# Gate and up with the first weight row's sign turned, s3 and s4 of the early pairs summed by accumulating transfers, and some changes in the mixers

## The chip, the cores and the metric

The kernel runs on one core of a Trainium2 chip. A core has a matrix engine (TensorE, PE), a vector engine (VectorE, DVE), an engine for activations and copies (ScalarE, ACT), a programmable one (GpSimd, POOL) and one that here only issues transfers (SyncE, SP). Each engine runs its own instructions in order and waits on semaphores for the others. Transfers issued by POOL can add to what stands in the destination; those issued by SP copy. The metric is the time of one execution on the device in microseconds (us).

## The reference

A two-layer encoder is applied to 512 + 256 tokens of width 1024 with shared weights. Cut to what matters:

```python
def rmsnorm(x, g):
    y = x32 * lax.rsqrt(jnp.mean(x32 * x32, axis=-1, keepdims=True) + EPS)
    return y.astype(x.dtype) * g
def swiglu(h, wg, wu, wd):
    return (jax.nn.silu(h @ wg) * (h @ wu)) @ wd
def even_layer(x, ...):
    x = x + 0.5 * swiglu(rmsnorm(x, f1_n), f1_g, f1_u, f1_d)
    x = x + mixer_ab(rmsnorm(x, mix_n), ...)
    x = x + 0.5 * swiglu(rmsnorm(x, f2_n), f2_g, f2_u, f2_d)
def odd_layer(x, ...):
    # the same with mixer_c in the middle
```

`mixer_ab` is a gated mixing of 128-token blocks (gelu, layer normalization, a 128x128 mixing matrix for each of four groups) beside attention in windows with 8 heads; `mixer_c` is attention in a 2-D neighbourhood with 16 heads and a bias from a table. The hidden width of the four FFNs (`swiglu`) is 2816. A normalization follows the last layer. All is float32.

## The kernel before

**Numbers.** A float32 product is made of three matmuls of a rounded type: each operand is split into `hi` (a cast on ScalarE, L125 for weights, L211 for activations) and `lo` (source minus hi, on VectorE, L126 and L212); then hi x hi, hi x lo and lo x hi are summed (`mm3`, L191).

**FFN.** The 768 tokens are two halves of 384. The hidden width is cut into 11 pairs of two 128-row blocks. For each pair, gate and up are made by a 2x2 scheme with seven instead of eight block products (Winograd's form of Strassen's): weight blocks a11 to a22 (columns of a pair's block i, upper or lower half of the 1024 inputs), activation blocks b11 to b22. The weight sums are s1 = a21 + a22, s2 = s1 - a11, s3 = a11 - a21, s4 = a12 - s2; the activation sums are t1 = b12 - b11, t2 = b22 - t1, t3 = b22 - b12, n4 = b21 - t2 (`feed_tmp`, `feed_t2`, `rest`, `combine`). The products are a11 b11, a12 b21, s2 t2, s3 t3, a22 n4, s1 t1, s4 b22. A product is 12 matmuls of 384 columns. The down projection (`down`, L797) uses the same scheme over two pairs at a time, with s3 of its own.

**Pairs and order.** The first four pairs (`EARLY`) of each FFN are split: their products a11 b11 and a12 b21 come first for all four, while the rest of the normalized input is still being made; the other five are done in `settle` (L681), pair after pair, in the order t2, t3, n4, t1, b22, gate then up. `entry` (L672) loads the weights of such a pair again, four transfers of 512 KB on SP, and `added` (L664) builds s1 by two transfers on POOL for each of gate and up, the second of which adds. s2, s3 and s4 are made by VectorE in `sums` (L771, at L773). `entry` of a pair runs at the end of the pair before it for pairs 1 and 2; for pair 3 it runs at its own start, after `down` of pairs 0 and 1 (L749). In the second FFN, the first after a mixer, L750 to L753 emit ahead of this point 60 transfers on POOL (L1668 and L1673: `skew`, 16 and 32, and `tab`, 8 and 4) that build the tables of the second mixer's bias.

**Order on the engines.** TensorE's order is that of the program. The other engines' orders are made by a scheduler when the program is built: of what is ready at a point of its own reckoning it takes what is earliest in the program, `high_priority` moves instructions ahead, and `issue_after` puts one behind another. On the chip each engine then follows its list strictly. Weight tiles `raw` have four buffers, sums `s` eight, `whi` and `wlo` five each.

**Mixers and norms.** `rsqrt` (L318) makes an inverse root either by about a dozen small VectorE instructions (L325 to L336) or, with `power`, by one on VectorE and one power on POOL (L322, L323). In the first mixer (L1158) `attention` and the gating run as side chains beside the projections: `turn` transposes and splits probabilities, `values` copies and adds halves of an output (L1282, L1288), `sgu` normalizes (L1350), splits, mixes and writes (L1359). Their results lie in four banks of the second accumulator pool (`ps_aux`).

Of the kernel before, what the change touches and what calls it, by code (L numbers as in the profile page):

```python
# [47 lines left out]
WTOTAL = 12 * D * FF + 16 * EARLY * P * D + D * 1792 + 2 * D * D + D * 3072 + D * 512  # L48
# [7 lines left out]
class Trunk:  # L56
# [43 lines left out]
    def raw(self, name, k0, nk, c0, n, raw=None, eng=None, **kw):  # L100
        i = len(self.units)
        self.units.append((name, k0, nk, c0, n))
        size = P * nk * n
        src = self.aps["w"][self.woff : self.woff + size].rearrange("(p f) -> p f", p=P)
        self.woff += size
        if raw is None:
            raw = self.rawp.tile([P, nk * n], F32, tag="raw", name=f"raw{i}")
        ins = (eng or self.nc.sync).dma_start(raw, src, **kw).ins  # L108
        if kw:
            self.added = ins  # L110
        else:
            self.loading = ins
        return raw.rearrange("p (k n) -> p k n", k=nk)
# [95 lines left out]
    def split(self, hi, lo, src, eng=None):  # L209
        nc = self.nc  # L210
        nc.scalar.copy(hi, src)  # L211
# [31 lines left out]
    def norm_tok(self, acc, c0, c1):  # L243
# [8 lines left out]
        self.rsqrt(y, ps[:, :nb], 1.0 / D, sm[:, 0, :nb], sm[:, 2, :nb], it[:, :nb])  # L252
# [9 lines left out]
    def tok_norm(self, h):  # L262
# [149 lines left out]
    def gain_split(self, n, k, src, m):  # L412

        hi, lo = self.b[n][k]
        ins = self.nc.scalar.activation(hi, src, AF.Copy, scale=self.gain(m)).ins
        self.fed = ins, self.nc.vector.scalar_tensor_tensor(
            out=lo, in0=src, scalar=self.gain(m), in1=hi.bitcast(F32), op0=ALU.mult, op1=ALU.subtract
        ).ins

    def combine(self, out, x, sign, m, other):  # L420

        g, op = (self.gain(m), ALU.subtract) if sign > 0 else (self.gain(m, self.ngains), ALU.add)
        self.nc.vector.scalar_tensor_tensor(out=out, in0=x, scalar=g, in1=other, op0=ALU.mult, op1=op)  # L423

    def rest(self, *after):
# [7 lines left out]
        for n in ("t3", "n4", "t1", "b22"):  # L433
            for k in range(4):
                with ExitStack() as stack:
                    for ins in self.holds:
                        stack.enter_context(self.tc.issue_after(ins))
                    if n == "t1":
                        self.gain_split(n, k, self.tmp[k], k)
# [4 lines left out]
                    elif n == "n4":  # L444
                        t = self.tmp["t2", k]
                        self.combine(t, self.x[k + 4][:, a0:a1], 1, k + 4, t)
# [48 lines left out]
    def ffn(self, pre):  # L495
# [49 lines left out]
        def pair(p):  # L545
# [15 lines left out]
            def sums(n, name):  # L561
                return self.sums(a[n, 1, 1], a[n, 1, 2], a[n, 2, 1], a[n, 2, 2], s, n, name)
# [39 lines left out]
            def hidden(i, half, g, u):  # L602
# [6 lines left out]
                nc.scalar.activation(t, t, AF.Silu)  # L609
                self.freed = nc.vector.tensor_tensor(out=v, in0=u, in1=r, op=ALU.mult).ins  # L610
                nc.vector.scalar_tensor_tensor(out=t, in0=t, scalar=0.5, in1=v, op0=ALU.mult, op1=ALU.mult)
# [51 lines left out]

            def added(then=None):  # L664
# [7 lines left out]
            def entry(ahead=False):  # L672
                if not loaded:
                    load((0, 1))
# [6 lines left out]
            def settle(st):  # L681
# [3 lines left out]
                for i, (n, b) in enumerate(todo):  # L685
# [14 lines left out]
                    if n == "up":  # L700
                        if b == "n4":
# [69 lines left out]
    def sums(self, a11, a12, a21, a22, s, n, name):  # L771
# [4 lines left out]
        if name == "s2" and (n, "s1") in s:  # L776
            t = s[n, "s2"] = self.fw.tile([P, 4, P], F32, tag="s", name="s2", bufs=8)
            f(t, s[n, "s1"], a11, ALU.subtract)
            return t
        if name == "s4":  # L780
            t = s[n, "s2"]
            f(t, a12, t, ALU.subtract)
# [5 lines left out]
        if name == "s3":  # L788
            f(t, a11, a21, ALU.subtract)
        else:  # L790
            f(t, s[n, "s1"], a11, ALU.subtract)
# [198 lines left out]
    def norm_r(self, mp, cols):  # L990
# [9 lines left out]
        self.ry = self.norm_tok(acc, 0, T)  # L1000
# [157 lines left out]
    def mixer0(self):  # L1158
# [104 lines left out]
        def turn(kv, n, blks, p):  # L1263
            res = []
            for i, b in enumerate(blks):
# [6 lines left out]
                res.append((th, tl))  # L1272
            return res

        def values(kv, n, blks, tt):
# [6 lines left out]
            nc.scalar.copy(tb, po[64:128, :])  # L1282
            for r in range(4):
                o = ot[4 + 2 * kv + r // 2]
                out, rows = o[r % 2 * 64 : r % 2 * 64 + 64, n * P : (n + 1) * P], lambda v: v
                if kv:
                    out, rows = self.by_column(o, slice(r % 2 * 64, r % 2 * 64 + 64), n * P, (n + 1) * P)
                nc.vector.tensor_tensor(  # L1288
                    out=out, in0=rows(po[0:64, r * P : (r + 1) * P]), in1=rows(tb[:, r * P : (r + 1) * P]), op=ALU.add
                )  # L1290
# [43 lines left out]
        def stats(vs):  # L1334
# [8 lines left out]
            self.rsqrt(y, mv[:, 0:3, 1], 1.0, nb, mv[:, 5, 0:3], it)  # L1343
# [3 lines left out]
        def sgu(n, v, y, nb):  # L1347

            i = n % 3
            nc.scalar.activation(v, v, AF.Identity, scale=y[:, i : i + 1], bias=nb[:, i : i + 1])  # L1350
            yield SGU[0] + i * SGU[1]
# [5 lines left out]
            for g in range(4):  # L1357
                c = slice(g * P, (g + 1) * P)
                nc.vector.scalar_tensor_tensor(  # L1359
                    out=ot[g][:, n * P : (n + 1) * P], in0=ps[:, c], scalar=lng[:, g : g + 1], in1=sb[:, c],  # L1360
                    op0=ALU.mult, op1=ALU.add,
                )
# [503 lines left out]
```

## Time and profile before

| what | value |
|---|---|
| median of three runs | 2585.51 us (2584.96 to 2587.59) |
| the profiled execution | 2584.44 us, its span 2582.7 us |
| mean granted TensorE clock | 0.997 |
| moved by transfers | 238.69 MB, of it 22.42 MB by POOL's queue |

A row of the page's groups gives line, engine, operation, output and input tiles, shape and count, then busy time, mean ns of one, and idle time of the engine just before it with what ended most of it. A row of the waits gives the engine and tile that waited, for whom, and the us in total, times, and longest. A row of the timeline gives start, length and the instruction, in brackets the idle time before it and who ended it. A row of stretches gives its bounds and length, then the busy time and count of PE, PEld, DVE, ACT and POOL, the granted clock, the share of the transfer engines and GB/s. The last number of a transfer's row is the time in us from issue to landing.

### The profile page before, as it was taken

Reading aid. Unit: us, or ns where it says so; the run is one execution under the profiler, and the core shown is the slowest. Engines: PE = TensorE matmul, PEld = TensorE weight load, DVE = VectorE, ACT = ScalarE, POOL = GpSimd, SP = SyncE. Lnnn points to the kernel's source line nnn. Section 1 sums busy time; section 2 is a strip of 40 time slices with the busy share of each in tenths; the row PEclk is TensorE's granted clock in tenths of the full one; section 3 lists DMA queues with packets and bytes.
Section 4 is the critical chain, followed back from the end, with each engine's and each line's share of the span. In section 5 each row is a group of like instructions: output and inputs, shape, how many; then the busy total and the mean of one; then the engine's idle time right before and its main releaser. Section 6 shows DMA issues by size and latency. Waiting matters only on the chain.

```text
span 2582.7 us, 41323 instructions
## 1 busy us (share of the span) xinstructions
PE 2549.8 (99%) x15114; PEld 2485.1 (96%) x15114; DVE 2229.4 (86%) x4650; ACT 1365.0 (53%) x2869; POOL 191.4 (7%) x318
## 2 busy tenths in 40 slices
PE   8999999999999999999999999999999999999998
PEld 8999999987899999999999999998998999999997
DVE  7988899888879889889998889986767699988897
ACT  7544454555656545445654445454545465444543
POOL 1000000000020500000100000001222220000000
PEclk9999999999999999999999999999999999999999
DMA  7422222421234722222532222242221343222222
GB/s 255 121 82 66 82 66 66 158 74 46 62 115 131 202 66 80 68 77 88 143 103 82 66 82 66 66 146 64 64 64 41 106 143 111 82 77 72 74 67 73
DMA packets 79422, 238.69 MB, mean 92 GB/s; under 512 B 9969, under 2 KB 18993, under 8 KB 79217
## 3 DMA queue, kind: packets, MB, share of 16 engines
q1 hardware_dynamic: 69136, 213.32, 25.9%
q0 software_dynamic: 9792, 22.42, 4.0%
q8 instruction: 119, 1.95, 0.3%
q14 instruction: 87, 0.70, 0.1%
q10 hardware_dynamic: 288, 0.29, 0.0%
HBM read 226.56 MB, written 15.07 MB: 94 GB/s over the span
## 4 chain that ended last, share of the span: by engine, by line
PE 88%; DVE 8%; ACT 2%; DMA 1%; issue 1%; DVEq 0%; ACTq 0%; POOL 0%; POOLq 0%
PE ps_mm L155 53%; PE ps_aux L155 33%; DVE wlo L126 1%; DMA raw<-in_w 1%; PE ps_aux L159 1%; ACT p L1143 1%; DVE p L1137 1%; DVE tmp L423 0%; DVE tl L212 0%; DVE p L1153 0%; ACT whi L125 0%; DVE s L773 0%; DVE o L1288 0%; DMA tok<-in_xt 0%; PE ps_aux L1719 0%
## 5 line engine op out<-in xcount | busy, mean ns | idle before, releaser
L125 ACT CAST whi<-s 128x512 fp32r<-128x512 f32 x496 | 304.7, 620 | 409.3 <-DVE s L773 185.8
L125 ACT CAST whi<-raw 128x512 fp32r<-128x512 f32 x504 | 306.5, 619 | 225.8 <-PE ps_mm L155 92.3
L126 DVE TENSOR_TENSOR wlo<-s,whi 128x512 fp32r<-128x512 f32 x496 | 337.6, 686 | 60.5 <-ACT whi L125 53.3
L126 DVE TENSOR_TENSOR wlo<-raw,whi 128x512 fp32r<-128x512 f32 x471 | 322.2, 693 | 20.1 <-ACT whi L125 16.8
L155 PE MATMUL ps_mm<-db,whi 128*128 128x384 f32 x864 | 219.1, 334 | 0.0
L155 PE MATMUL ps_aux<-dt,whi 128*128 128x384 f32 x864 | 219.1, 334 | 0.0
L155 PEld LDWEIGHTS ps_aux<-dt,whi 128*128 128x128 f32 x864 | 156.0, 188 | 0.0
L155 PEld LDWEIGHTS ps_mm<-db,whi 128*128 128x128 f32 x864 | 156.0, 188 | 0.0
L155 PE MATMUL ps_mm<-xh,whi 128*128 128x512 f32 (+1 forms) x416 | 145.6, 350 | 0.0
L155 PE MATMUL ps_aux<-dt,wlo 128*128 128x384 f32 x432 | 144.3, 334 | 0.0
L155 PE MATMUL ps_mm<-db,wlo 128*128 128x384 f32 x432 | 144.3, 334 | 0.0
L155 PE MATMUL ps_mm<-xh,wlo 128*128 128x512 f32 (+1 forms) x416 | 140.9, 339 | 0.0
L155 PE MATMUL ps_mm<-xl,whi 128*128 128x512 f32 (+1 forms) x416 | 140.7, 338 | 0.0
L773 DVE TENSOR_TENSOR s<-raw,raw 128x512 f32<-128x512 f32 x124 | 84.1, 686 | 29.0 <-DMA raw<-in_w 28.8
L599 DVE TENSOR_TENSOR u<-ps_aux,u 128x384 f32<-128x384 f32 x176 | 97.2, 552 | 3.2 <-PE ps_aux L155 2.6
L155 PE MATMUL ps_aux<-dh,whi 128*128 128x384 f32 x384 | 97.5, 334 | 0.0
L126 POOL TENSOR_TENSOR wlo<-raw,whi 128x512 fp32r<-128x512 f32 x33 | 43.8, 1335 | 714.4 <-DVE p L1153 581.8
L829 DVE TENSOR_TENSOR x<-ps_aux,x 128x384 f32<-128x384 f32 x160 | 85.2, 552 | 13.1 <-PE ps_aux L155 13.0
L1143 ACT ACTIVATE p<-p,st 128x256 f32<-128x256 f32 (+3 forms) x144 | 68.9, 480 | 48.3 <-DVE st L1141 48.3
L108 POOL DMA_DIRECT2D s<-in_w x64 | 46.9, 782 | 620.6 <-PE ps_aux L155 339.7
L829 DVE TENSOR_TENSOR x<-ps_mm,x 128x384 f32<-128x384 f32 x160 | 85.9, 551 | 5.2 <-PE ps_mm L155 5.0
L594 ACT COPY u<-ps_mm 128x384 f32<-128x384 f32 x176 | 83.5, 474 | 12.2 <-PE ps_mm L155 11.8
(522 smaller groups left out, 8204.3 us busy)
## 6 DMA issues: line engine op xcount, KB each, us to landing
raw<-in_w SPq DMA_DIRECT2D x346, 512.0 KB, 3.7
s<-in_w POOLq DMA_DIRECT2D x64, 256.0 KB, 4.6
xdm<-x SPq DMA_DIRECT2D x16, 384.0 KB, 2.4
x<-in_x SPq DMA_DIRECT2D x16, 192.0 KB, 4.8
tok<-in_xt SPq DMA_DIRECT2D x12, 256.0 KB, 6.2
xold<-xdm SPq DMA_DIRECT2D x8, 384.0 KB, 3.1
x<-xdm SPq DMA_DIRECT2D x8, 384.0 KB, 4.8
out_y<-y SPq DMA_DIRECT2D x8, 384.0 KB, 2.5
```

What stands on the lines that cost most here:

```text
L108: ins = (eng or self.nc.sync).dma_start(raw, src, **kw).ins
L125: self.cast = nc.scalar.copy(hi, src).ins
L126: (eng or nc.gpsimd).tensor_tensor(out=lo, in0=src, in1=hi.bitcast(F32), op=ALU.subtract)
L155: self.nc.tensor.matmul(out, lhsT=lhsT, rhs=rhs, start=start, stop=stop, **kw)
L159: self.nc.tensor.transpose(out, src, self.ident)
L594: nc.scalar.copy(e[n, out], bank[key, n])
L599: nc.vector.tensor_tensor(out=t, in0=bank[key, n], in1=t, op=ALU.add)
L773: f = lambda o, x, y, op: self.nc.vector.tensor_tensor(out=o, in0=x, in1=y, op=op)
L829: nc.vector.tensor_tensor(out=o, in0=ps, in1=o, op=ALU.add)
L1137: nc.vector.tensor_tensor_reduce(out=outs[i], in0=ps_list[i], in1=adds[i], scale=1.0, scalar=init[i], op0=ALU.add, op1=ALU.max, accum_out= ...
L1143: ins = nc.scalar.activation(outs[i], outs[i], AF.Exp, bias=nm[:, i : i + 1], accum_out=sm[:, i : i + 1])
```

## The change

With a11 and a12 taken as their negatives, the first row of the product has its sign turned and all four weight sums become additions: s2 = s1 + a11, s3 = a11 + a21, s4 = a12 + s2. t1, t2 and n4 get the other sign, and where a result belongs to the turned row the activation and the factor take -1 and -0.5. In the early pairs s3 is now built in a `raw` tile (a21 loaded on SP, a11 added by a transfer on POOL), and s4 by a transfer on POOL that adds a12 to the tile of s2 once that has been split; only s2 is left to VectorE. The loads of `entry` become pieces of 256 KB (`settled`). Beside this, three more callers of the inverse root use the power, the output writes of the first mixer get high priority, and the normalization in `sgu` is put behind the next turn's last cast.

```diff
-    def norm_tok(self, acc, c0, c1):
+    def norm_tok(self, acc, c0, c1, power=False):
...
-            self.rsqrt(y, a, 1.0 / D, a, b, it[:, :3], h == 0)
+            self.rsqrt(y, a, 1.0 / D, a, b, it[:, :3], True)
...
-        self.combine(t2, self.tmp[k], -1, k, self.tmp[k + 4])
+        self.combine(t2, self.tmp[k], 1, k, self.tmp[k + 4])
...
             def sums(n, name):
-                return self.sums(a[n, 1, 1], a[n, 1, 2], a[n, 2, 1], a[n, 2, 2], s, n, name)
+                if early and name in ("s3", "s4"):
+                    return s[n, name]
+                return self.sums(*(a.get((n, i, j)) for i in (1, 2) for j in (1, 2)), s, n, name, ALU.add)
...
-                nc.scalar.activation(t, t, AF.Silu)
+                nc.scalar.activation(t, t, AF.Silu, scale=-1.0 if i else 1.0)
...
+            def piece(n, i, k, to, eng=None, **kw):
+                self.raw(f"{pre}_w_{n}", k, 4, (2 * p + i) * P, P, to.rearrange("p a b -> p (a b)"), eng, **kw)
+
+            def settled():
+                three, *rest = (
+                    self.rawp.tile([P, KD * P], F32, tag="raw", name="three").rearrange("p (k n) -> p k n", k=KD)
+                    for _ in range(3)
+                )
+                for i, n in enumerate(names):
+                    a[n, 1, 1], a[n, 2, 2] = rest[i][:, 0:4, :], rest[i][:, 4:8, :]
+                    s[n, "s3"] = three[:, 4 * i : 4 * i + 4, :]
+                    piece(n, 0, 0, a[n, 1, 1])
+                    piece(n, 1, 0, s[n, "s3"])
+                for n in names:
+                    piece(n, 0, 0, s[n, "s3"], nc.gpsimd, accum_op=ALU.add)
+                    piece(n, 1, 4, a[n, 2, 2])
+
+            def fourth():
+                for n in names:
+                    s[n, "s4"] = s[n, "s2"]
+                    piece(n, 0, 4, s[n, "s4"], nc.gpsimd, accum_op=ALU.add)
...
                 if not loaded:
-                    load((0, 1))
+                    settled()
...
                     if n == "up":
+                        if b == "t2":
+                            fourth()
...
-        self.ry = self.norm_tok(acc, 0, T)
+        self.ry = self.norm_tok(acc, 0, T, True)
...
-            nc.scalar.copy(tb, po[64:128, :])
+            with self.tc.high_priority():
+                nc.scalar.copy(tb, po[64:128, :])
...
-            self.rsqrt(y, mv[:, 0:3, 1], 1.0, nb, mv[:, 5, 0:3], it)
+            self.rsqrt(y, mv[:, 0:3, 1], 1.0, nb, mv[:, 5, 0:3], it, True)
...
-            nc.scalar.activation(v, v, AF.Identity, scale=y[:, i : i + 1], bias=nb[:, i : i + 1])
-            yield SGU[0] + i * SGU[1]
+            t, old = self.t, self.turned
+            while self.turned is old and self.t < t + 0.75 * SGU[0]:
+                yield 0.2
+            with self.tc.issue_after(self.turned):
+                nc.scalar.activation(v, v, AF.Identity, scale=y[:, i : i + 1], bias=nb[:, i : i + 1])
+            yield max(SGU[0] + i * SGU[1] + t - self.t, 0.2)
```

The adds of L1288 and the writes of L1359 are put under `high_priority` in the same way as the copy `tb`.

More of the change, by code (lines that the diff above doesn't have):

```diff
@@ L769, in ffn, with sums @@
             self.close("work")
-    def sums(self, a11, a12, a21, a22, s, n, name):
+    def sums(self, a11, a12, a21, a22, s, n, name, sign=ALU.subtract):
         f = lambda o, x, y, op: self.nc.vector.tensor_tensor(out=o, in0=x, in1=y, op=op)
@@ L788, in sums @@
         if name == "s3":
-            f(t, a11, a21, ALU.subtract)
+            f(t, a11, a21, sign)
         else:
-            f(t, s[n, "s1"], a11, ALU.subtract)
+            f(t, s[n, "s1"], a11, sign)
         return t
```

45 lines of the change are left out of this document (25 added, 20 removed).

## The prediction

> **What bounds the kernel now.** I read the page's busy times first, then the waits of TensorE over the whole run, then single stretches.
>
> ```profile
> PE 2549.8 (99%) x15114; PEld 2485.1 (96%) x15114; DVE 2229.4 (86%) x4650; ACT 1365.0 (53%) x2869; POOL 191.4 (7%) x318
> ```
> ```profile
> PE ps_aux L155 <- DVE tl L212: 4.6, 8, 1.4
> PE ps_mm L155 <- DVE wlo L126: 3.8, 7, 0.7
> PE ps_mm L155 <- ACT whi L125: 2.4, 3, 1.6
> ```
> ```profile
> 36.00:76.00 40.00, 32.49 (x169) 28.37 (x168) 38.58 (x90) 24.73 (x60) 6.45 (x10) 1.00 0.62 171
> 76.00:470.00 394.00, 394.00 (x2273) 393.54 (x2272) 357.16 (x655) 199.88 (x398) 2.90 (x4) 1.00 0.26 81
> ```
>
> TensorE is busy in 2549.8 of 2582.7 us, and its longest kinds of wait are a few us each. The last two rows are stretches (PE, PEld, DVE, ACT, POOL busy, clock, DMA share, GB/s). From 76 to 470 us TensorE never stops: VectorE work taken away there is worth nothing. From 36 to 76 us, the early pairs of the first FFN, VectorE works 38.58 of 40 us and TensorE loses 7.5 us. So the change can only earn at a few places; its matrix products are the same number and size, and removing every idle us would give 33 us at most.
>
> **What the sign turn and the sums cost.** Scales and add instead of subtract change an operand, not a duration: nothing. In the 16 early pairs four 128x512 sums per pair (s3 and s4, gate and up) leave VectorE:
>
> ```profile
> L773 DVE TENSOR_TENSOR s<-raw,raw 128x512 f32<-128x512 f32 x124 | 84.1, 686 | 29.0 <-DMA raw<-in_w 28.8
> ```
>
> That is 64 x 0.686 = 44 us of VectorE, almost all under a busy TensorE, where it earns 0. In exchange POOL issues four more transfers per pair, and each pair loads a11 and a21 for s3 as pieces of half the size: cheap on SP, whose queue is not on the chain.
>
> **Where the sums earn: the first FFN.**
>
> ```profile
> 49.51 0.68 DVE L773 TENSOR_TENSOR s<-raw,raw 128x512 f32<-128x512 f32 x1
> 50.11 0.15 DVE L334 TENSOR_TENSOR sm<-sm 128x3 f32<-128x3 f32 x1
> ...
> 52.14 0.15 DVE L334 TENSOR_TENSOR sm<-sm 128x3 f32<-128x3 f32 x1
> 52.21 0.55 DVE L212 TENSOR_TENSOR n40l<-tmp,n40h 128x384 fp32r<-128x384 f32 x1
> ```
> ```profile
> 50.92 0.45 PE L155 MATMUL ps_mm<-t30h,whi 128*128 128x384 f32 x1 [1.55 <-ACT whi L125]
> ```
> ```profile
> PE ps_aux L155 <- DVE b223l L212: 1.4, 1, 1.4
> ```
>
> VectorE goes from one instruction to the next without a gap, so what counts is start to start: 0.60 us for a sum (49.51 to 50.11), 0.07 for a step of the Newton root (52.14 to 52.21). TensorE waits 1.55 us for the cast of s3, which stood behind VectorE's backlog. Removed ahead of TensorE's wait for b223l: two s3 and two s4 (4 x 0.60 = 2.4 us) and about eleven Newton steps (0.8 us). As VectorE is the limit of this stretch, I take all of it: **-3.2 us** (bounds 0, if the casts on ScalarE are late instead, and -7.5, the whole loss). The transfers that replace s3 are issued by POOL some 10 us ahead of their use and hide; if that cover went, the same wait of 1.55 us would come back.
>
> In the other early stretches only one wait for wlo, behind such a sum, is seen: 0.5 us in 770 to 910 us and 0.6 in 2090 to 2180.
>
> ```profile
> PE ps_mm L155 <- DVE wlo L126: 0.5, 1, 0.5
> ```
> ```profile
> PE ps_mm L155 <- DVE wlo L126: 0.6, 1, 0.6
> ```
>
> **-1.1 us** (bounds 0 and -2.5, with issue time and the waits for s4 beside them).
>
> **The mixers.** The rows are of the first mixer: VectorE, then TensorE, then stretches.
>
> ```profile
> 570.65 0.16 DVE L334 TENSOR_TENSOR mv<-mv 128x3 f32<-128x3 f32 x1
> 570.73 0.68 DVE L212 TENSOR_TENSOR tl<-ps_aux,th 128x512 fp32r<-128x512 f32 x1
> ...
> 585.22 0.34 DVE L1359 SCALAR_TENSOR_TENSOR o<-ps_aux,lng,sb 128x128 f32<-128x128 f32 x1
> ...
> 586.98 1.16 DVE L1288 TENSOR_TENSOR o<-ps_aux,tb 64x128 f32<-64x128 f32 x4
> ```
> ```profile
> 587.12 0.66 PE L159 MATMUL ps_aux<-ident,p 128*128 128x128 f32 x4 [1.66 <-DVE o L1359]
> 588.29 0.30 PE L155 MATMUL ps_aux<-swh,vhh 128*128 128x128 f32 x1 [0.52 <-DVE o L1288]
> ```
> ```profile
> 590.00:596.80 6.80, 6.80 (x30) 5.50 (x30) 5.64 (x20) 0.13 (x1) 0.00 (x0) 0.50 0.22 77
> 627.50:631.00 3.50, 3.50 (x10) 2.68 (x10) 3.50 (x16) 0.65 (x2) 0.00 (x0) 0.51 0.00 0
> ```
>
> Power instead of Newton frees VectorE between 569 and 572 us, where tl, which gives back the banks, stands behind it: -0.5. High priority for L1359 and L1288 draws together what is now strung out over 585.2 to 588.1 between other work: of 1.66 + 0.52 us I take -1.7. After these waits the granted clock is 0.50 for 6.8 us and 0.51 for 3.5: 10.3 us at half speed lose 5.1. If the waits shrink a stretch may disappear: bounds 0 and -5.1, I take -1.7, the shorter one. The gate's normalization now waits for the next turn's cast; in the second half of the mixer that puts three activations behind it and can make TensorE late: bounds 0 and +2, I take +0.5. Sum **-3.4 us**.
>
> The Trainium skill, TensorE: Matmul & The Clock Gate, section What's actually happening, says that the gate goes to half rate after at least one idle window of about 3.4 us and to full after a busy one. The trace does not agree on the first: waits of 1.66 and 0.52 us were enough here. By the page alone all the -1.7 would be 0 here, and the sum 1.7 us higher.
>
> In the second mixer POOL adds biases:
>
> ```profile
> 1737.00 3.20 POOL L1464 TENSOR_TENSOR add<-ba,mb 128x192 f32<-128x192 f32 x4 [5.71 <-DVE mb L1451]
> 1742.02 0.67 POOL L1464 TENSOR_TENSOR add<-ba,mb 128x192 f32<-128x192 f32 x1 [1.82 <-DVE sm L334]
> ```
> ```profile
> 1739.41 0.82 DVE L326 TENSOR_SCALAR smi<-sm 128x6 int32<-128x6 int32 x1
> ```
> ```profile
> 1745.76 1.53 PE L155 MATMUL ps_aux<-diag,onesr 128*128 128x384 f32 x4 [0.95 <-DVE diag L312]
> ```
> ```profile
> L323 POOL TENSOR_TENSOR sm<-sm,space 128x3 f32<-128x3 f32 x1 | 0.9, 899 | 14.7 <-DVE sm L322 14.7
> ```
>
> The power (0.9 us) fits POOL's gap from 1740.2 to 1742.0; then the diagonals are some 2 us sooner and the wait goes: **-0.9 us**. If it stands behind the later adds (to 1745.4), the diagonals come about 2 us later: +2. In the gap is likelier, as only the adds that need the second cast of mb stand there.
>
> The Trainium skill, SBUF — State Buffer, section Who interferes with whom, speaks against moving work to POOL: a VectorE operation with two SBUF inputs and a GpSimd one that reads SBUF block each other. The row of 0.82 us for a 6-element step fits it in kind; for one power of 0.9 us it would take at most 0.9 from the gain.
>
> **What it may cost: POOL's queue at pair 3 of the second FFN.** There 60 transfers that build the bias tables stand ahead of pair 3 in the program, on POOL. First POOL, then TensorE, then landing times, cast and pace.
>
> ```profile
> 852.32 6.10 POOL L1668 DMA_DIRECT2D skew<-in_rpb  x11 [0.93 <-issue]
> 860.18 3.93 POOL L1673 DMA_DIRECT2D tab<-skew  x7 [1.76 <-DMA skew<-in_rpb]
> ...
> 877.54 7.85 POOL L1668 DMA_DIRECT2D skew<-in_rpb  x14 [0.42 <-issue]
> 887.82 1.91 POOL L1673 DMA_DIRECT2D tab<-skew  x3 [2.43 <-DMA skew<-in_rpb]
> 895.76 0.63 POOL L1673 DMA_DIRECT2D tab<-skew  x1 [6.03 <-issue]
> ```
> ```profile
> 888.21 0.33 PE L155 MATMUL ps_mm<-t30h,whi 128*128 128x384 f32 x1
> ```
> ```profile
> s<-in_w POOLq DMA_DIRECT2D x8, 256.0 KB, 4.8
> ```
> ```profile
> L125 ACT CAST whi<-s 128x512 fp32r<-128x512 f32 x496 | 304.7, 620 | 409.3 <-DVE s L773 185.8
> ```
> ```profile
> 834.22 12.48 PE ps_mm L155 x72
> ```
>
> Before the change pair 3 needs nothing of POOL. After it both s3 have an accumulating transfer on POOL, emitted behind the tables. A ready table transfer comes first; only where a tab waits for the skews (the gap up to 887.82) can a later one slip in, and that gap was one transfer wide before: the first 16 skews are one table, the eleven of 852.32 end with the 17th, and the tabs follow at 860.18. So I put gate's s3 there and up's behind the last tab: issued at 895.76 + 0.63 = 896.4, landed 4.8 us later at 901.2, cast in 0.62: 901.8, and 0.4 more for wlo. TensorE starts gate's t3 at 888.2; a product is 12 of the 72 matmuls in 12.48 us, 2.08 us, so up's is due at 890.3. It waits 901.8 + 0.4 - 890.3 = **+12 us**. Queued behind POOL there are then only pair 3's s4 transfers, due 10 us later. The idle time brings the half clock: with the row at 590 us, 6.8 us at 0.50 lose **+3.4**. Together +15.4; bounds 0 (both ahead of the tables) and +19 (both behind, with a transfer slowed by the tabs ahead of it in the queue). In the FFNs without tables the same transfers have a free POOL: 0.
>
> **Sum.** -3.2 - 1.1 - 3.4 - 0.9 + 15.4 = +6.8 us. On the profiled execution (2584.44 us; span 2582.7 and 1.7 around it) that is 2591.2; the median of the runs shown, 2585.51, lies 1.1 us above, so I forecast **2592 us**. By the bounds this case spans 2584 to 2599.
>
> **Rivals.**
> 1. *The order on POOL lets s3 through*, because its loads are ready early and the tables are not: +0 instead of +15.4, so 2585.5 - 8.6 = 2577 us. For it: the order isn't written out, and the 17th skew overtook the first tab. Against it: that skew was the next in the same list. This one ends faster. Chance 0.25.
> 2. *Both s3 slip into the one gap*: gate's is issued at about 885.4, lands at 890.8 with its issue, and TensorE waits 890.8 + 0.6 - 888.2 = 3.2 us: 2580 us. Chance 0.15.
> 3. *The jam, and the stretches don't give their gain*: in the first FFN ScalarE's casts take VectorE's place, in the mixers the new order makes new waits. +15.4 and -2: 2599 us. Decides where ScalarE's wait at 50.9 stays although its sum is gone. Chance 0.15.
> 4. *The forecast*, 0.45.
> That the sums don't leave VectorE can't be: they aren't issued.
>
> **Range and chances.** About 0.2% (5 us) is what a measurement of this kernel can tell from no change. Faster by more: most of rival 1 and half of rival 2, 0.32. Slower by more: rival 3 and half of the forecast, 0.38. Within: 0.30. The range 2575 to 2600 holds rivals and forecast with one tenth on either side.
>
> **What would show it.** Right: POOL's s<-in_w behind the last tab near 896 us, TensorE idle there for 10 us or more with a clock near 0.5 after it; 76 to 470 us unchanged; the losses of 36 to 76 us down by about 3 us; no wait on L1359 at 587. Wrong: s3's transfers ahead of the tabs, or new waits for raw or s tiles in the early pairs.

## The result

| kernel | median of the runs | before, beside it | ratio to before, 95% interval |
|---|---|---|---|
| after | 2616.78 us (2614.39 to 2617.81) | 2586.55 us | 1.0117 [1.0105, 1.0129] |

The change makes the kernel slower by about 30 us, 1.2%. The forecast was 2592 us, 6.5 us slower than before, in a range of 2575 to 2600: the sign was right, the size and the range were not.

The page of after, in the lines that answer to those of before (busy time of each engine, the software queue, which is POOL's, and the landing of the transfers):

```profile
PE 2563.0 (98%) x15114; PEld 2497.5 (96%) x15114; DVE 2189.4 (84%) x4526; ACT 1365.6 (52%) x2869; POOL 252.4 (10%) x387
...
q0 software_dynamic: 19008, 39.20, 8.2%
...
three<-in_w POOLq DMA_DIRECT2D x32, 256.0 KB, 5.7
```

VectorE works 40 us less (2229.4 to 2189.4), as the 64 sums are gone. POOL's queue moves 39.20 MB in place of 22.42. And TensorE, with the same 15114 matmuls, is done 30 us later. The waits of TensorE over the whole run of after (who waited for whom: us in total, times, longest):

```profile
PE ps_mm L155 <- ACT u L598: 11.0, 4, 4.8
PE ps_mm L155 <- ACT whi L125: 4.8, 3, 2.8
PE ps_mm L155 <- ACT p L628: 3.9, 2, 3.4
...
PE ps_aux L155 <- ACT whi L125: 2.6, 1, 2.6
PE ps_aux L155 <- DVE u L603: 2.1, 2, 1.9
```

The first row is new in kind: `u` of L598 is no weight but a copy of a result, which has nothing to do with the sums. Something else holds ScalarE. Its four waits are at t3 in each of the four FFNs: 4.8 us at 57, 2.6 at 828, 2.6 at 1312 and 1.0 at 2170.

To see where the time went I took every matmul's start, up to the start of the next one, less the usual distance of its size (0.173 us for 384 columns), and added that up by stage. The stages are bounded by the same matmuls in each kernel. This is worked out from the traces, in us that TensorE loses by waits and by half clock:

```
stage (us of before)      before  after  vector_sums  tables_later  s2_behind  s2_tables  all_mended
first FFN     0-100        15.7   20.7      17.8         21.0         20.1       21.9       15.7
first mixer   520-720      11.1   14.9      13.4         13.0         15.0       13.4       10.5
2nd FFN p0-2  720-850       2.5    6.1       2.5          6.6          2.5        1.8        2.0
2nd FFN p3    850-960       1.3   13.7       0.7          1.3         13.9        0.6        1.2
third FFN     1250-1345     0.3    5.5       0.2          6.7          0.8        0.7        0.9
second mixer  1680-2090     2.3    0.7       1.3          2.5          0.7        0.7        0.5
fourth FFN    2090-2215     2.5    4.2       2.9          6.7          4.6        2.9        2.8
whole run                  40.9   70.9      43.8         62.7         62.6       47.1       39.1
```

The columns after the second are experiments told below. Each column is one profiled execution; a stage whose code was not touched still differs by 1 to 2 us between kernels, in the fourth FFN up to 4. One stretch of half clock of 3.4 us more or less makes 1.7 us of this.

**Pairs 0 to 2 of the second FFN.** VectorE of after (start, length, instruction, in brackets the idle time before it and who ended it):

```profile
817.31 0.56 DVE L603 TENSOR_TENSOR u<-ps_aux,u 128x384 f32<-128x384 f32 x1 [0.40 <-PE ps_aux L155]
822.90 0.69 DVE L801 TENSOR_TENSOR s<-s,three 128x512 f32<-128x512 f32 x1 [5.03 <-DMA s<-in_w]
823.51 0.55 DVE L614 TENSOR_TENSOR u<-u,acc 128x384 f32<-128x384 f32 x1
...
826.12 0.55 DVE L612 TENSOR_TENSOR u<-u,acc 128x384 f32<-128x384 f32 x1
```

POOL, ScalarE and TensorE at the same place:

```profile
811.22 1.73 POOL L108 DMA_DIRECT2D three<-in_w  x2 [7.33 <-DVE b223l L212]
812.59 1.49 POOL L108 DMA_DIRECT2D s<-in_w  x2
818.62 3.57 POOL L108 DMA_DIRECT2D s<-in_w  x4 [4.53 <-DMA s<-in_w]
```
```profile
826.70 0.52 ACT L613 ACTIVATE u<-u 128x384 f32<-128x384 f32 x1 [4.74 <-DVE u L612]
827.13 0.60 ACT L125 CAST whi<-three 128x512 fp32r<-128x512 f32 x1
827.64 0.47 ACT L598 COPY u<-ps_mm 128x384 f32<-128x384 f32 x1
```
```profile
828.16 0.44 PE L155 MATMUL ps_mm<-t30h,whi 128*128 128x384 f32 x1 [2.56 <-ACT u L598]
```

Read from the bottom: TensorE waits 2.56 us for the copy of u2 at 827.64. That copy stands on ScalarE behind the activation of L613, which waits 4.74 us for VectorE's L612. And VectorE has stood still for 5.03 us in front of a sum, s2 of gate of **pair 2**, which no matmul needs until 846. Its source s1 comes by the transfers of 812.59 and 818.62 (the adding ones wait 4.53 us for the copying ones to land), and these stand on POOL behind s3's transfers of pair 1 (811.22). What those wait for is named by POOL's row in the third FFN, where s1's transfers follow in the same way: the load of a21 into the tile of s3.

```profile
1290.59 1.76 POOL L108 DMA_DIRECT2D three<-in_w  x2 [27.73 <-DMA three<-in_w]
1292.05 1.43 POOL L108 DMA_DIRECT2D s<-in_w  x2
```

So three engines, each strict in its order, pass one late landing on to TensorE. Over the whole run such waits are:

```profile
DVE s L801 <- DMA s<-in_w: 11.5, 3, 5.0
...
DVE s L801 <- DMA three<-in_w: 7.8, 8, 2.3
```

Before has none of the first row. Another of these waits (3.0 us) is in the third FFN, where TensorE then loses 5.5 us.

**Pair 3 of the second FFN.** POOL, then TensorE:

```profile
882.84 11.10 POOL L1704 DMA_DIRECT2D skew<-in_rpb  x20 [0.27 <-issue]
894.48 3.90 POOL L1704 DMA_DIRECT2D skew<-in_rpb  x7 [0.53 <-issue]
898.42 1.82 POOL L108 DMA_DIRECT2D three<-in_w  x2
899.61 1.51 POOL L108 DMA_DIRECT2D s<-in_w  x1
900.90 1.56 POOL L1709 DMA_DIRECT2D tab<-skew  x2
...
907.89 0.96 POOL L108 DMA_DIRECT2D s<-in_w  x1
```
```profile
903.50 0.45 PE L155 MATMUL ps_mm<-t30h,whi 128*128 128x384 f32 x1 [2.78 <-ACT whi L125]
...
920.01 0.44 PE L155 MATMUL ps_aux<-b220h,whi 128*128 128x384 f32 x1 [1.93 <-DVE u L603]
...
926.02 0.69 PE L155 MATMUL ps_aux<-b220h,whi 128*128 128x384 f32 x1 [2.65 <-ACT whi L125]
```

The queue is there as forecast: s3's two transfers come behind all the skews, s4's second one behind the last tab. But both s3 slip in ahead of the tabs, so the wait at t3 is 2.8 us and not 12. Two waits in front of b22 follow, and the clock falls (bounds, length, busy time of the engines, granted clock): 0.83 over 40 us, 6.8 us lost. The three waits make 7.4 us.

```profile
900.00:940.00 40.00, 32.53 (x155) 30.84 (x154) 27.90 (x51) 17.01 (x34) 4.66 (x7) 0.83 0.48 132
```

**The first FFN.** Before, then after, in the same 9 us (the last two numbers: share of the transfer engines, GB/s); then ScalarE and TensorE of after:

```profile
33.00:42.00 9.00, 7.79 (x45) 7.47 (x44) 7.95 (x16) 7.94 (x20) 0.32 (x1) 1.00 1.04 297
```
```profile
33.00:42.00 9.00, 5.61 (x30) 5.29 (x29) 7.24 (x15) 5.72 (x14) 3.04 (x4) 0.91 0.96 213
```
```profile
39.27 0.63 ACT L275 ACTIVATE tok<-tok 128x512 f32<-128x512 f32 x1 [2.29 <-DMA tok<-in_xt]
...
40.30 0.47 ACT L628 COPY p<-ps_mm 128x384 f32<-128x384 f32 x1
```
```profile
40.82 0.69 PE L155 MATMUL ps_mm<-b210h,whi 128*128 128x384 f32 x1 [3.39 <-ACT p L628]
```

The transfer engines are nearly as busy as before but move 213 in place of 297 GB/s, the input tokens come later, and behind their activation stands the copy that TensorE waits for.

### The profile page after: what moved, and what is told of

The parts are those of the page before. It is cut to its first block, busy times and chain, and to the rows that moved or that the text cites. A ratio compares the mean times of both kernels' runs of the same rounds, so it can differ in the third digit from the quotient of the medians.

```text
span 2612.6 us, 41390 instructions
## 1 busy us (share of the span) xinstructions
PE 2563.0 (98%) x15114; PEld 2497.5 (96%) x15114; DVE 2189.4 (84%) x4526; ACT 1365.6 (52%) x2869; POOL 252.4 (10%) x387
## 3 DMA queue, kind: packets, MB, share of 16 engines
q0 software_dynamic: 19008, 39.20, 8.2%
## 4 chain that ended last, share of the span: by engine, by line
PE 45%; DVE 2%; ACT 1%; DMA 1%; issue 1%; POOL 0%; DVEq 0%; ACTq 0%; POOLq 0%
PE ps_mm L155 28%; PE ps_aux L155 17%; PE ps_aux L159 1%; ACT p L1171 0%; DMA three<-in_w 0%; DVE wlo L126 0%; DVE p L1165 0%; DVE p L1181 0%; DMA raw<-in_w 0%; DMA s<-in_w 0%; DVE tl L212 0%; DVE qk L1653 0%; DVE y L340 0%; DVE st L1169 0%; DVE acc L238 0%
## 5 line engine op out<-in xcount | busy, mean ns | idle before, releaser
L125 ACT CAST whi<-s 128x512 fp32r<-128x512 f32 x464 | 285.0, 620 | 381.6 <-PE ps_mm L155 123.3
L125 ACT CAST whi<-raw 128x512 fp32r<-128x512 f32 x472 | 286.9, 618 | 228.9 <-PE ps_mm L155 95.7
L126 DVE TENSOR_TENSOR wlo<-s,whi 128x512 fp32r<-128x512 f32 x464 | 315.4, 685 | 74.6 <-ACT whi L125 64.4
L126 DVE TENSOR_TENSOR wlo<-raw,whi 128x512 fp32r<-128x512 f32 x439 | 300.8, 692 | 18.6 <-ACT whi L125 15.0
L108 POOL DMA_DIRECT2D s<-in_w x96 | 78.8, 955 | 568.8 <-PE ps_aux L155 349.0
L613 ACT ACTIVATE u<-u 128x384 f32<-128x384 f32 x88 | 46.2, 525 | 82.7 <-DVE u L612 82.7
L155 PEld LDWEIGHTS ps_mm<-xh,whi 128*128 128x128 f32 x416 | 79.3, 191 | 9.1 <-issue 1.0
L155 PEld LDWEIGHTS ps_mm<-xh,wlo 128*128 128x128 f32 x416 | 79.1, 190 | 8.6
```

What stands on the lines that cost most here:

```text
L125: self.cast = nc.scalar.copy(hi, src).ins
L126: (eng or nc.gpsimd).tensor_tensor(out=lo, in0=src, in1=hi.bitcast(F32), op=ALU.subtract)
L155: self.nc.tensor.matmul(out, lhsT=lhsT, rhs=rhs, start=start, stop=stop, **kw)
L613: nc.scalar.activation(t, t, AF.Silu, scale=-1.0 if i else 1.0)
```

## Experiments

The theory after this reading, called A below: the transfers cost by their place in POOL's strict order, and VectorE's and ScalarE's own strict orders pass the lateness on. The main rival, B: the turned sign and the new order of all lists cost. Lines in the experiments are shifted by up to four against after.

| kernel | median us | before beside it | ratio, 95% interval |
|---|---|---|---|
| sign_alone | 2586.09 | 2586.12 | 1.0002 [0.9993, 1.0011] |
| mixers_alone | 2588.70 | 2585.33 | 1.0014 [1.0005, 1.0023] |
| vector_sums | 2588.59 | 2585.33 | 1.0015 [1.0006, 1.0024] |
| s3_alone | 2600.38 | 2586.12 | 1.0053 [1.0039, 1.0066] |
| s4_alone | 2601.56 | 2585.71 | 1.0071 [1.0057, 1.0085] |
| tables_later | 2604.11 | 2585.33 | 1.0074 [1.0060, 1.0087] |
| s1_sooner | 2612.70 | 2585.33 | 1.0108 [1.0094, 1.0121] |
| mended | 2593.55 | 2585.71 | 1.0030 [1.0019, 1.0042] |
| s2_behind | 2607.62 | 2586.54 | 1.0086 [1.0071, 1.0101] |
| s2_tables | 2591.75 | 2586.54 | 1.0021 [1.0012, 1.0029] |
| s4_s2_behind | 2601.00 | 2586.54 | 1.0056 [1.0042, 1.0070] |
| priority_alone | 2585.86 | 2585.71 | 1.0003 [0.9993, 1.0013] |
| one_power | 2585.18 | 2585.71 | 0.9999 [0.9990, 1.0008] |
| hold_alone | 2585.01 | 2586.12 | 0.9996 [0.9987, 1.0005] |
| second_root | 2588.83 | 2586.12 | 1.0005 [0.9996, 1.0014] |
| all_mended | 2580.84 | 2586.31 | 0.9978 [0.9969, 0.9987] |
| mended_vector | 2581.19 | 2585.57 | 0.9985 [0.9974, 0.9996] |

### Which part of the change costs

**vector_sums**: after with s3 and s4 on VectorE.

```diff
             def sums(n, name):
-                if early and name in ("s3", "s4"):
-                    return s[n, name]
...
-                    settled()
+                    load((0, 1))
...
-                        if b == "t2":
-                            fourth()
```

> After with s3 and s4 of the early pairs added by VectorE again (loads as before, no transfers for them on POOL); sign turn and the changes in the mixers and norms stay. Theory A (the transfers' place in POOL's strict order is what costs, because VectorE and ScalarE wait for them in their own strict order): the 16 us that TensorE loses more in the second FFN, 5.3 in the third and 2.3 in the fourth go, 0 to 5 of the first FFN too: 2588 to 2593 us. Theory B (the sign turn and the scheduler's other order of casts and copies cost, whoever adds): over 2605 us, with PE <- ACT u still among the waits of the second and third FFN.

2588.59 us, as theory A had it. Against after the transfers cost 0.0102 of 2586 us, 26 us. The losses of the second, third and fourth FFN are back at before's.

**sign_alone**: before with the turned sign and additions on VectorE (of the change's diff only the scales, the gains and `ALU.add` in `sums`).

> Before with only the turned sign: additions instead of subtractions in the sums of gate and up, all on VectorE. Both theories: no instruction more or longer, 2585 to 2586 us. If the other order of the lists that the scheduler makes of it costs anything, 2588 us or more.

No difference. B has fallen.

**mixers_alone**: before with the rest of the change (the powers, the high priority and the part of `sgu` in its diff, nothing in the FFNs' products).

> Before with only the changes outside the seven products: three more roots by power, high priority for the first mixer's output writes, the normalization in the gating behind the next turn's last cast. Theory A (the root of the first norm is late only because it stands behind waiting transfers on POOL): first mixer about +2.4, second mixer -1.5, first FFN 0 to +2: 2586 to 2590 us. Rival C (the root on POOL is itself the cost in the first FFN): first FFN +4 or more there, 2590 to 2593 us.

1.0014: 3.6 us slower. The stages say +3.8 in the first mixer, -1.6 in the second, +2.2 in the fourth FFN and 0.6 in the first, where the wait at t3 is 3.2 us but others are shorter. Rival C, 4 us or more in the first FFN, has fallen.

**s3_alone** and **s4_alone**: after with only one of the two sums by transfers. In s3_alone `settled` has a fourth raw tile `last`:

```diff
-                if early and name in ("s3", "s4"):
+                if early and name == "s3":
...
+                    a[n, 1, 2] = last[:, 4 * i : 4 * i + 4, :]
+                    piece(n, 0, 4, a[n, 1, 2])
...
-                            fourth()
```

and s4_alone:

```diff
-                if early and name in ("s3", "s4"):
+                if early and name == "s4":
...
-                    settled()
+                    load((0, 1))
```

> After with s4 added by VectorE again and only s3 by transfers on POOL (a12 loaded on SP as two pieces of 256 KB). Theory A: s3's transfers stand ahead of s1's and behind the tables' skews, so the stalls near 37, 825, 900 and 1310 us stay: 2588.6 plus 12 to 20, 2601 to 2609 us. If the costs of s3 and s4 add, 2604 us (28 minus the 13 that s4 alone cost). If s4 is the greater part and s3 costs only in company with it: under 2598 us.

> After with s3 added by VectorE again (loads in tiles of 512 KB as before) and only s4 by transfers on POOL. Theory A (place in POOL's queue): nothing of s3's stands ahead of s1 any more, so the stalls near 825 and 1310 us and that near 37 us go; at pair 3 of the second FFN the two s4 transfers still stand behind the tables' skews and come a few us late, with half clock: 2588.6 (VectorE adds all) plus 3 to 9, so 2592 to 2598 us. Rival D' (s3 and s4 share the 28 us evenly): near 2602 us.

Over vector_sums s3 costs 0.0038 and s4 0.0056, 10 and 14 us: they nearly add up to 26. (The intervals overlap; which of the two costs more can't be told.) So s3 came out a little below the 12 to 20 of theory A, and s4, which theory A thought cheap, costs about as much; rival D' was right there.

Of the four stalls that were to stay in s3_alone only the one at 900 does. At 37 us the wait is 1.2 us as in before (a new one, of 4.2 us at t2, is at 47), and near 825 and 1310 there is none: TensorE loses 1.7 us in pairs 0 to 2 of the second FFN and 1.4 in the third, where after loses 6.1 and 5.5. Yet s1 of pair 2 stands on POOL behind s3 of pair 1 as in after and is as late there. POOL, then VectorE, in s3_alone:

```profile
817.29 1.78 POOL L108 DMA_DIRECT2D s<-in_w  x2 [6.30 <-DMA s<-in_w]
```
```profile
825.67 0.68 DVE L802 TENSOR_TENSOR s<-s,three 128x512 f32<-128x512 f32 x1
```

The sum s2 of pair 2 comes at 825.67 without a wait, behind the sums of s4 that VectorE makes here. In after, where VectorE is rid of those, the same sum was next at 817.9 and waited 5.03 us. So the place on POOL alone does not make these stalls: the sum has to have moved forward on VectorE too, and it has done so where the sums of s4 have left VectorE.

At pair 3 of the second FFN s3_alone waits 2.6 us at t3 and has no wait of more than 0.4 us in front of b22; s4_alone has none at t3 and waits of 2.2 and 0.7 us in front of b22. So what after loses in front of b22 comes with s4's transfers behind the tables, and not from the wait at t3. On ScalarE of after the cast of s4 at 925.37 stands behind an activation that waits 3.49 us for VectorE; why it stands there was not followed further.

### Which place costs

**tables_later**: after with the bias tables behind pair 3.

```diff
-                if mixed and p == 2 and self.spare:
...
+            if mixed and p == 3 and self.spare:
+                with self.tc.issue_after(self.added):
+                    while self.spare:
+                        self.spare.pop(0)()
```

> After with the 60 transfers of the bias tables emitted behind pair 3 of the second FFN instead of ahead of it. Theory A (queue on POOL): the wait of 2.9 us at 900 goes, and the ones of 2.1 and 3.0 at 918 and 923 and the half clock of 900 to 940 with it, as they are its followers: -12 to -14, so 2603 to 2605 us. Rival E (the ones at 918 and 923 come from VectorE's own backlog with pair 4's sums): only -4 to -5, 2612 us.

2604.11 us, 0.0043 or 11 us less than after. TensorE's waits in 860 to 940 us are then one of 0.2 us:

```profile
PE ps_aux L155 <- DVE u L603: 0.2, 1, 0.2
```

So the waits at 920 and 926 go with the tables too, and E does not explain them.

**s1_sooner**: s1 of the next pair ahead of s3 of the pair in hand.

```diff
+                if not p:
+                    addeds[1](behind + 3 if fresh else None)
                 now = entered.pop(p, None) or entry()
...
+                        if not p:
+                            addeds[2]()
                         entered[p + 1] = entries[p + 1]()
```

> After with the four s1 transfers of the next pair issued ahead of the s3 transfers of the pair in hand (pairs 1 and 2). Theory A: VectorE's waits in s2 for s<-in_w (11.5 us in three waits) go, and with them the stalls of TensorE near 825 us (2.7 and 1.7 of half clock), 1310 us (5.3 with clock) and 2169 us (1.1 to 2): 2604 to 2609 us. Rival D (s3's own transfers are late, through the free raw tile that their load waits for): TensorE's stalls stay, 2614 us or more.

2612.70 us, only 2 us less than after: a miss. The stalls at 825 and 1310 are gone (third FFN 5.5 to 1.0), but new ones are there at 781 and 2121 us (2.8 and 3.8 us), and pair 3 of the second FFN loses 17.1 us where after loses 13.7. ScalarE and the transfers issued in 760 to 786 us (count, size, median us to landing), in s1_sooner:

```profile
778.18 0.62 ACT L125 CAST whi<-raw 128x512 fp32r<-128x512 f32 x1 [3.61 <-DMA raw<-in_w]
```
```profile
s<-in_w POOLq DMA_DIRECT2D x8, 256.0 KB, 6.4
raw<-in_w SPq DMA_DIRECT2D x4, 512.0 KB, 6.3
```

After issues four of the former there, and its four loads of 512 KB land in 3.9 us. Moved forward, the transfers run beside the loads that the next casts need, and those land later.

**s2_behind**: POOL as in after; only VectorE's list is changed.

```diff
                 if ahead:
                     return None
+                if p in (1, 2):
+                    s["hold"] = self.freed
...
+                with self.tc.issue_after(s["hold"]) if name == "s2" and "hold" in s else nullcontext():
+                    return self.sums(...)
```

> After with one thing changed: the sum s2 of pairs 1 and 2 is put, on VectorE, behind the second last hidden product of the pair before (issue_after), where it was drawn up to 14 us ahead of its use. POOL's order stays as in after. Theory H (VectorE's list: a sum whose source lands late stands ahead of work that TensorE needs): the stalls near 825 us (2.7) and 1310 us (2.7) go with their half clock and the one near 2169 shrinks, -7 to -11: 2606 to 2610 us. Theory A in its narrow form (only s1's lateness on POOL counts, wherever VectorE reads it): the wait only moves to t2 of the next pair, 2613 us or more.

2607.62 us, 0.0031 or 8 us less than after. VectorE's waits in the sums now have no row for s<-in_w:

```profile
DVE s L804 <- DMA raw<-in_w: 37.5, 57, 2.7
...
DVE s L804 <- DMA three<-in_w: 3.8, 5, 2.0
```

The transfers are no earlier (those that add to s1 of pair 2 are issued at 821.22, in after at 818.62); the late sum no longer stands in front of anything. Theory H is right for the second and third FFN, whose losses go from 6.1 to 2.5 and from 5.5 to 0.8. The fourth shows nothing of it (4.2 and 4.6).

**s2_tables**: the edits of s2_behind and tables_later.

> The same, and the bias tables behind pair 3 of the second FFN (2604 us without the first). Theory H: 2593 to 2598 us, as the two causes lie in different stretches. Theory A narrow: 2601 us or more.

2591.75 us, 0.0096 or 25 us less than after, a little better than expected and more than the two alone (8 and 11). What it still loses over before is in the first FFN and the first mixer.

**mended**: the edits of s1_sooner and tables_later, and two more.

```diff
-            self.rsqrt(y, a, 1.0 / D, a, b, it[:, :3], True)
+            self.rsqrt(y, a, 1.0 / D, a, b, it[:, :3], h == 0)
...
-                    settled()
+                    load((0, 1)) if fresh and not p else settled()
```

> After with four things mended: s1's transfers ahead of s3's, the bias tables behind pair 3, pair 0 of the first FFN with s3 by VectorE, and the second root of the first norm on VectorE. Theory A: first FFN back to about before (5 less than after), second FFN 15 less, third 4 to 5 less: 2590 to 2596 us. If something of the transfers costs that has nothing to do with their place (more traffic, slower landing), 2600 us or more.

2593.55 us, as expected. TensorE's wait for the copy of L628 near 37 us is 1.2 us in place of 3.4.

**s4_s2_behind**: the edits of s4_alone and s2_behind.

> s4_alone (2601.6 us) with s2 of pairs 1 and 2 put behind in the same way. Theory H: there too a sum s2 that waits (3.3 us on VectorE near 83 us) holds casts that TensorE needs; that goes, 2594 to 2598 us. If s4's transfers cost by their own landing, 2600 us or more.

2601.00 us, against the 2594 to 2598 of H. Where s4_alone had the waiting sum, the wait of 2.7 us in front of t3 at 85 us goes, and the first FFN loses 16.8 us in place of 21.7. But the waits in front of b22, s4's own product, grow from 4.7 us (1.2, 2.2, 1.3) to 7.3 (1.8, 3.0, 1.4, 1.1): pair 3 of the second FFN loses 6.5 in place of 3.6, the fourth FFN 7.6 in place of 4.2. The transfers of 815 to 826 us, and ScalarE:

```profile
raw<-in_w SPq DMA_DIRECT2D x4, 512.0 KB, 7.7
s<-in_w POOLq DMA_DIRECT2D x4, 256.0 KB, 9.7
```
```profile
832.36 0.62 ACT L125 CAST whi<-s 128x512 fp32r<-128x512 f32 x1 [3.74 <-DMA s<-in_w]
```

The four transfers on POOL, of s1 and s4, start when s2 has been split, from 817.9 us, and four loads of 512 KB start at 819.7; the four land after 9.7 us in the median. In s2_tables, where s3's and a12's part of the loads is gone, the same window has three loads of 256 KB, which start at 824.8, 4 us behind POOL's, and the four land after:

```profile
s<-in_w POOLq DMA_DIRECT2D x4, 256.0 KB, 5.8
```

That would explain why s4 alone costs as much as s3 alone, but it is not shown: a run that parts the loads from s4 was not made.

### The mixers and the norms

**priority_alone**, **one_power**, **hold_alone**, **second_root**: before with one of these four parts of the change's diff: the high priority in `values` and `sgu`, `norm_tok(acc, 0, T, True)`, the lines of `sgu` with `self.turned`, and `True` for `h == 0` in L278.

> Before with only the high priority of the first mixer's four kinds of output writes. Theory F (the writes drawn forward push other work of VectorE and ScalarE back, so a new wait of 1.9 us near 589 and 2.8 near 637 takes the old one's place): the first mixer loses as much or up to 4 us more, 2585 to 2589 us. Theory G (the new waits come from the held normalization in the gating): here the first mixer gains as the prediction had it, 2582 to 2584 us.

> Before with only the root ahead of each mixer by power on POOL. The second mixer's wait for diag near 1746 us goes (-0.9 to -1.6), the first mixer stays: 2584 to 2585 us. If the first mixer's loss comes from this root: +2 or more, 2587 us.

> Before with only the gating's normalization put behind the next turn's last cast. If the hold is the rest of the first mixer's loss (high priority alone left the time the same, all the changes of mixers and norms together cost 3.4 us): 2587 to 2589 us, with waits of TensorE near 590 or 640 us that before doesn't have. If not, 2585 to 2586 us.

> Before with only the second root of the first norm by power on POOL. If the stall at t3 of the first FFN (1.7 us in before, 3.3 with all the changes of mixers and norms) comes from the root, it is 3 us or more here and the time 2586 to 2588 us; if it comes from elsewhere, about 1.7 and 2585 us or less.

None of the four can be told from before by its ratio; the largest are second_root (+1.3 us, by the medians +2.7) and priority_alone (+0.8). priority_alone lies where F had it and not where G had it; hold_alone shows no cost of the hold. TensorE's waits in 580 to 645 us, before, then mixers_alone:

```profile
PE ps_aux L159 <- DVE o L1359: 1.7, 1, 1.7
PE ps_aux L155 <- DVE tl L212: 1.4, 1, 1.4
PE ps_aux L155 <- DVE o L1288: 0.5, 1, 0.5
```
```profile
PE ps_aux L159 <- DVE p L1153: 2.8, 3, 1.4
PE ps_aux L155 <- DVE o L1291: 1.7, 1, 1.7
PE ps_aux L155 <- DVE tl L212: 0.2, 1, 0.2
```

The wait for L1359 is gone as forecast, and waits of the same size for other work of VectorE are there. In one_power the wait for diag in the second mixer is gone. In second_root the wait at t3 of the first FFN is 3.25 us in place of 1.55: the power stands on POOL behind four transfers, the last of which waits for a landing.

```profile
47.99 0.89 POOL L108 DMA_DIRECT2D s<-in_w  x1 [1.62 <-DMA s<-in_w]
49.37 0.88 POOL L108 DMA_DIRECT2D s<-in_w  x1 [0.48 <-DMA s<-in_w]
49.95 1.23 POOL L323 TENSOR_TENSOR sm<-sm,space 128x3 f32<-128x3 f32 x1
```

### A version that beats both

**all_mended**: the edits of s2_tables, the two of mended's own diff, and no high priority in the first mixer. **mended_vector**: after with the edit of vector_sums, the root of mended's diff (`h == 0`), and no high priority.

> s2_tables with three more things put back: s3 of pair 0 of the first FFN by VectorE, the second root of the first norm on VectorE, no high priority in the first mixer. If these are what is left (s2_tables 2591.8 us): first FFN -4 to -5, first mixer -2, second mixer keeps its gain of 1.5, so 2583 to 2586 us, at or just below before. If the transfers keep a cost that their place doesn't explain, 2588 us or more.

> The same as all_mended, but s3 and s4 added by VectorE (no transfers for them, tables and s2 where they were). If all_mended's gain of 5.5 us over before comes from the transfers, this stands 3 us or more above it, 2584 to 2586 us; if it comes from the rest (the roots by power in the mixers, the hold), it is as fast, 2580 to 2582 us.

all_mended is 5.5 us faster than before (0.9978 [0.9969, 0.9987]), 2 us below the range that was expected, and 36 us faster than after. But mended_vector is as fast: the intervals overlap, and the medians differ by 0.35 us. That points to what the two have in common (the powers in the mixers, the hold, the turned sign) and not to the transfers. Which of these gives the gain is not shown: none that was run alone shows it by itself, the power in the gating was not run alone, and in the profiled executions TensorE loses only 1.8 us less in all_mended than in before, as much as in the second mixer alone. Once nobody waits for them, some 43 us less work on VectorE (62 of the 64 sums) are worth nothing that these runs can tell.

## Why the prediction was wrong

- **The sign turn: right.** It was put at 0 and sign_alone shows 0.
- **"In the FFNs without tables the same transfers have a free POOL: 0": this step failed.** It looked at what stands ahead of s3 on POOL, not at what s3 then stands ahead of: s1 of the next pair, which is read by s2. And it took the 44 us that leave VectorE as worth 0, where they moved s2 forward in VectorE's list, in front of work that TensorE was due (s3_alone has the same order on POOL, but not this, and no such stall). The early pairs lose 3.6 us more in pairs 0 to 2 of the second FFN, 5.2 in the third and 1.7 in the fourth, where the forecast had -1.1; s2_behind shows the cause for the first two, the fourth is within the spread.
- **First FFN, -3.2: this step failed too.** It came out at +5.0. "As VectorE is the limit of this stretch, I take all of it" left out ScalarE and the transfers: from 33 to 42 us of before ScalarE works 7.94 of 9 us and the share of the transfer engines is 1.04. The wait of 3.4 us at 40.8 goes with s3's transfers of pair 0 (1.2 in mended and in s4_alone), the longer one at t3 comes in part from the root behind transfers (second_root). No kernel here loses less than before's 15.7 us there: all_mended, which keeps s3 of pair 0 and the root on VectorE, loses as much, and s3_alone, with both off VectorE, 18.8.
- **The queue at pair 3: the jam is there, the parts were others, and that the sum is near is in part luck.** The term was +15.4: one wait of 12, and 3.4 by the clock. The stage loses 12.4 more (13.7 less 1.3), and tables_later takes 11 us off the time. But both s3 passed ahead of the last tabs, the order of rival 2 (its price was 3.2, the wait is 2.8). "Queued behind POOL there are then only pair 3's s4 transfers, due 10 us later" put those at nothing; the waits of 1.9 and 2.7 in front of b22 come with them (s4_alone has such waits, s3_alone has none). And the half clock costs 6.8 us, twice what was put.
- **First mixer, -3.4: failed.** +3.8 in after and in mixers_alone: the high priority changed who is waited for. The -1.7 for the clock had no ground in the rows: the shorter stretch, at 627.5, stands 39 us behind the waits at 587 and 588 and follows another, of 1.44 us for tl at 625.6. In after both stretches are still there, and the first is longer (593.4 to 603.6 us at 0.50), which is 1.7 of the 3.8. priority_alone loses 1.9 more there, but so does second_root, which changes nothing in the mixer; how much of the rest is spread stays open.
- **Second mixer, -0.9: right.** The power stood in the gap as forecast, though it took 1.35 us on six columns (the 0.9 was of three), and the wait for diag is gone; the stage loses 1.6 us less. The row of 0.82 us that was set beside operations with two inputs has a single one (L326); a row with two is L335 at 1742.05, 0.66 us where the one at 1740.67 took 0.17, beside POOL's add of 0.67 at 1742.02.
- **The range** ended at 2600, just above rival 3, and not by the bounds of the terms: the upper ones (+19 at pair 3, +2 for the diagonals, +2 for the held normalization, no gain by the clock or in the FFNs) add up, with the -0.5 and -1.7 that had none, to +20.8, some 2606 us. The step that failed had no bound at all, since it was set to 0. Rival 3 (2599 us) came nearest, and its sign was there, a wait at t3 of the first FFN that stayed (1.55 us, then 4.84). Both signs of being wrong came too: s3 ahead of the tabs, and new waits for s tiles.

By stage the difference is 5.0 + 3.8 + 3.6 + 12.4 + 5.2 - 1.6 + 1.7 = 30.1 us, against 30.0 in TensorE's total. Against the forecast's +6.8 that is 23.3 us more: 11.6 from the early pairs behind the first FFN, 8.2 from the first FFN, 7.2 from the first mixer, and 3.0 and 0.7 less from pair 3 and the second mixer.

## What to carry to other kernels

Work moved from a busy engine to a queue is not free because the queue is idle: ask what stands behind it there, which landing each of these waits for, and where their readers stand in the strict list of every other engine. A reader that was put early, because an engine has become free, holds everything behind it when its source is late; put it behind the work that is due first. And a term set to 0 needs a bound like any other.

## What the runs showed of the hardware

- With accumulating transfers in flight the transfer engines were nearly as busy and moved less: shares of 1.04 and 0.96, but 297 and 213 GB/s in the same 9 us of the first FFN. (The pieces are smaller there too; the adding by itself was not measured.) A transfer of 256 KB on POOL lands in 4.7 to 5.7 us in the median of after, in 9.7 us beside four loads of 512 KB (s4_s2_behind). The Trainium skill, DMA: Bandwidth & Descriptors, section Anatomy of one DMA — SWDGE (gpsimd) path, gives about 2.0 us plus bytes / 436e3 for a transfer issued by GpSimd, an estimate of 2.6 us for this size; the traces do not agree for these, of which half or more add and many overlap with others; none was measured alone.
- After a wait of 2.56 us TensorE ran at half clock for 3.4 us (in after):

```profile
828.80:832.20 3.40, 3.40 (x12) 3.40 (x12) 2.00 (x5) 1.30 (x4) 1.75 (x2) 0.52 0.90 283
```

  The Trainium skill, TensorE: Matmul & The Clock Gate, section What's actually happening, has a free-running window of about 3.4 us. The length agrees, and before's 3.5 and 6.8 us are one and two of them; that a whole idle window is needed first does not agree.
